# A streaming SiLU-times-multiply kernel: load and store rings exchanged, and the first load issued ahead of the preamble's barrier

## The chip, the cores and the metric

The kernel runs on one core of a Trainium2 chip. The metric is the device time of one execution in microseconds (us).

The engines named are ACT (ScalarE, the SiLU), DVE (VectorE, the multiply) and SP (SyncE, which here only issues DMAs). In the profile, what SP issues is on the ring q1 and what ACT issues on q10: the 134.22 MB of loads are on q1 before, where SP issues them. The profile counts 16 DMA engines. "A DMA engine" below is one of these 16. A transfer has 16 landing records in the trace, which I take as one from each; a packet (one piece of a transfer) has a record of its ring, time and size, but not of the DMA engine that carried it.

## The reference

```python
x: float32 [32, 512, 2048]
x1, x2 = x[..., :1024], x[..., 1024:]
out = x1 * (1 / (1 + np.exp(-x1))) * x2      # float32 [32, 512, 1024]
```

134.2 MB are read and 67.1 MB written.

## The kernel before

The 16,384 rows are cut into 16 tiles of 128 partitions by 8 rows. A tile is loaded by one DMA of 8 MiB, computed in four pieces, and stored by one DMA of 4 MiB. Both pools have two buffers. Loads are issued by SP, stores by ACT. The last tile is stored in four pieces of 1 MiB as its pieces are done. The framework schedules the instructions; it may place those of one engine in another order than the program's.

```python
in_pool  = ctx.enter_context(tc.tile_pool(name="in_pool", bufs=2))
out_pool = ctx.enter_context(tc.tile_pool(name="out_pool", bufs=2))
def load(i):
    xt = in_pool.tile([P, K, in_cols], dt, name="xt")        # K = 8
    nc.sync.dma_start(out=xt, in_=xv[i])                     # L45
    loaded[i] = xt
load(0); load(1)
for i in range(n_tiles):                                     # 16
    ...
    for c in range(0, K, KC):                                # KC = 2
        ce = c + KC
        nc.scalar.activation(out=ot[:, c:ce, :], in_=xt[:, c:ce, :half], func=Silu)    # L56
        nc.vector.tensor_mul(out=ot[:, c:ce, :], in0=ot[:, c:ce, :], in1=xt[:, c:ce, half:])  # L61
        if last:
            nc.scalar.dma_start(out=ov[i][:, c:ce, :], in_=ot[:, c:ce, :])             # L67
    if not last:
        nc.scalar.dma_start(out=ov[i], in_=ot)                                         # L69
    if i + 2 < n_tiles:
        load(i + 2)
```

## Time and profile before

| | before |
|---|---|
| time, median of the first 3 runs | 472.03 us (471.82 to 472.82) |
| span in the profile | 470.1 us |
| bytes moved, mean rate over the span | 201.35 MB, 428 GB/s |
| first load issued / its first packet | 0.73 / 1.73 us |
| load 15 has landed | 451.97 us |
| last store issued / last packet ends / last landing | 465.37 / 468.88 / 469.22 us |

The page of the kernel before: the span, the busy time of the compute engines, the DMA engines' busy tenths in 40 slices, and the rings (packets, MB, share of the 16 engines' span).

```profile
span 470.1 us, 267 instructions
...
DVE 142.4 (30%) x64; ACT 118.3 (25%) x65; POOL 0.2 (0%) x4
...
DMA  8999999999999999999999999999999999999998
...
q1 hardware_dynamic: 2304, 134.22, 66.2%
q10 hardware_dynamic: 2736, 67.11, 33.1%
q14 instruction: 2, 0.02, 0.0%
```

DVE and ACT are busy 30% and 25%; the DMA engines are at nine tenths or more in 38 of 40 slices. Loads are on q1 (SP), stores on q10 (ACT). This kernel is bound by the DMA engines.

The chain of waits that ended last, cut to one period (start, length, what):

```profile
347.05 47.10 DMA xt<-in_x_dram
...
394.23 1.92 ACT ot L56
...
396.18 8.91 DVE ot L61 x4
...
405.10 46.87 DMA xt<-in_x_dram
```

One should not read this as "47 us of load, then 11 us of compute that nobody hides". The next load (405.10) is issued when the compute frees its buffer, but another load is still running then, and so is a store. The chain shows what releases what. That the DMA engines are never empty in the middle is read from the next view: busy shares by stretch (share of the 16 DMA engines and GB/s stand last; a packet is counted whole where it starts, so a share can pass 1).

```profile
core 0: us, DVE busy (x) ACT busy (x) POOL busy (x), PEclk, DMA share, GB/s
60.00:440.00 380.00, 115.67 (x52) 95.02 (x52) 0.00 (x0) 1.00 1.00 434
462.00:464.80 2.80, 1.75 (x1) 1.01 (x1) 0.00 (x0) 1.00 1.01 427
464.80:466.80 2.00, 0.54 (x1) 0.00 (x0) 0.00 (x0) 1.00 0.54 225
466.80:468.90 2.10, 0.00 (x0) 0.00 (x0) 0.00 (x0) 1.00 0.91 375
```

In the 380 us of the middle the share is 1.00 at 434 GB/s. The dip is in the tail: 0.54 in the two microseconds from 464.8.

The timeline of the head (SP issues loads 0 and 1, in one merged line), and of the last tile:

```profile
0.73 0.85 SPq L45 DMA_DIRECT2D xt<-in_x_dram  x2
```

```profile
452.05 5.51 ACT L56 ACTIVATE ot<-xt 128x2048 f32<-128x2048 f32 x3 [21.65 <-DMA xt<-in_x_dram]
453.99 6.70 DVE L61 TENSOR_TENSOR ot<-ot,xt 128x2048 f32<-128x2048 f32 x3 [20.06 <-ACT ot L56]
456.32 4.74 ACTq L67 DMA_DIRECT2D out_dram<-ot  x3
461.11 1.91 ACT L56 ACTIVATE ot<-xt 128x2048 f32<-128x2048 f32 x1 [3.54 <-DVE ot L61]
463.05 2.29 DVE L61 TENSOR_TENSOR ot<-ot,xt 128x2048 f32<-128x2048 f32 x1 [2.36 <-ACT ot L56]
465.37 0.34 ACTq L67 DMA_DIRECT2D out_dram<-ot  x1
```

The framework put three of the last tile's stores between ACT's third and fourth ACTIVATE. Each store waits for a multiply of DVE, so ACT stands still for 3.54 us, DVE then for 2.36 us, and the last store goes out late. ACT's waits say the same:

```profile
ACT ot L56 <- DMA xt<-in_x_dram: 340.4, 16, 21.9
ACT ot L56 <- DVE ot L61: 3.5, 1, 3.5
...
```

### The profile page before, as it was taken

The page shows a single profiled execution, that of the slowest core. Times are in us where ns is not written, and L with a number is a line of the kernel's source. Part 1 is how long each engine was busy: PE and PEld are TensorE (multiplying, and loading weights), DVE is VectorE, ACT ScalarE, POOL GpSimd, SP SyncE. Part 2 cuts the span into 40 slices and gives each one's busy share as a digit, 9 for nine tenths or more (in the row PEclk, how much of TensorE's full clock was granted, in tenths as well). Part 3 has the DMA queues.
Part 4 walks back from the last instruction along what each step waited for, and adds up shares of the span by engine and source line. Part 5 has one row for each costly group of instructions (what it writes and reads, how often), then busy time and mean ns, then how long its engine had stood idle before and what let it go on. Part 6 is the DMA issues. An engine that isn't in the chain of part 4 may idle for free.

```text
span 470.1 us, 267 instructions
## 1 busy us (share of the span) xinstructions
DVE 142.4 (30%) x64; ACT 118.3 (25%) x65; POOL 0.2 (0%) x4
## 2 busy tenths in 40 slices
DVE  0070704207052070511606115070250702407033
ACT  1050506014060240602306032060320604106041
POOL 0000000000000000000000000000000000000000
DMA  8999999999999999999999999999999999999998
GB/s 357 446 446 401 401 485 435 418 401 443 449 446 401 441 457 396 446 474 390 468 404 438 457 441 407 427 420 449 446 410 432 480 401 418 440 474 424 399 424 337
DMA packets 5042, 201.35 MB, mean 428 GB/s; under 512 B 560, under 2 KB 560, under 8 KB 560
## 3 DMA queue, kind: packets, MB, share of 16 engines
q1 hardware_dynamic: 2304, 134.22, 66.2%
q10 hardware_dynamic: 2736, 67.11, 33.1%
q14 instruction: 2, 0.02, 0.0%
HBM read 134.22 MB, written 67.11 MB: 428 GB/s over the span
## 4 chain that ended last, share of the span: by engine, by line
DMA 80%; DVE 15%; ACT 4%; issue 0%; ACTq 0%; SPq 0%
DMA xt<-in_x_dram 80%; DVE ot L61 15%; ACT ot L56 4%; SPq L45 0%; ACTq L67 0%; ACTq L56 0%
## 5 line engine op out<-in xcount | busy, mean ns | idle before, releaser
L61 DVE TENSOR_TENSOR ot<-ot,xt 128x2048 f32<-128x2048 f32 x64 | 142.4, 2286 | 322.9 <-ACT ot L56 322.9
L56 ACT ACTIVATE ot<-xt 128x2048 f32<-128x2048 f32 x64 | 117.1, 1898 | 344.0 <-DMA xt<-in_x_dram 340.4
L56 ACT ACT_TABLE_LOAD x1 | 1.3, 1283 | 0.7 <-PEq L86 0.7
L86 POOL MEMSET const-bfloat16-1.0<- 128x1 bf16 x1 | 0.1, 101 | 0.0
L86 POOL MEMSET const-uint8-127<- 128x1 uint8 x1 | 0.1, 101 | 0.0
L86 POOL MEMSET const-float32-0.0<- 128x1 f32 x1 | 0.1, 98 | 0.2 <-issue 0.2
L86 POOL MEMSET const-float32-1.0<- 128x1 f32 x1 | 0.1, 98 | 0.0
## 6 DMA issues: line engine op xcount, KB each, us to landing
out_dram<-ot ACTq DMA_DIRECT2D x15, 4096.0 KB, 39.7
out_dram<-ot ACTq DMA_DIRECT2D x4, 1024.0 KB, 5.4
xt<-in_x_dram SPq DMA_DIRECT2D x16, 47.1
```

The source lines that it names most:

```text
L56: nc.scalar.activation(out=ot[:, c:ce, :], in_=xt[:, c:ce, :half], func=mybir.ActivationFunctionType.Silu,)
L61: nc.vector.tensor_mul(out=ot[:, c:ce, :], in0=ot[:, c:ce, :], in1=xt[:, c:ce, half:],)
L86: nc = _bacc.Bacc("TRN2", target_bir_lowering=False, num_devices=1)
```

## The change

The program begins with a preamble, which ends in a barrier at which the engines wait for one another (in the trace before, SP and ACT each wait 0.7 us there, for PE last, and go on at 0.65 us); each engine has a drain instruction before it, from 0.00 us (SP) and 0.13 us (ACT) to 0.32 us (PE). The change's intent: (1) start the first transfer before that barrier, (2) take the stores off ACT, so that a store that waits no longer holds up an ACTIVATE. Loads go to ACT, stores to SP, the order is kept as written, and a hook moves the first load ahead of ACT's drain in the preamble. The `PLAN` list only gives every tile the same 8 rows as before.

```diff
+def issue_ahead_of_the_first_barrier(nc):
+    head, body = nc.main_func.blocks[:2]
+    load = next(ins for ins in body.instructions if type(ins).__name__ == "InstDMACopy")
+    at = next(
+        j for j, ins in enumerate(head.instructions)
+        if ins.engine == load.engine and type(ins).__name__ == "InstDrain"
+    )
+    body.instructions = [ins for ins in body.instructions if ins.name != load.name]
+    head.instructions = head.instructions[:at] + [load] + head.instructions[at:]
...
+    nc.at_finalize(issue_ahead_of_the_first_barrier)
+    ctx.enter_context(tc.manual_schedule())
...
-        nc.sync.dma_start(out=xt, in_=xv[i])
+        nc.scalar.dma_start(out=xt[:, :plan[i][1], :], in_=view(x_flat, i))
...
-                nc.scalar.dma_start(out=ov[i][:, c:ce, :], in_=ot[:, c:ce, :])
+                nc.sync.dma_start(out=ov[:, c:ce, :], in_=ot[:, c:ce, :])
...
-            nc.scalar.dma_start(out=ov[i], in_=ot)
+            nc.sync.dma_start(out=ov, in_=ot[:, :k, :])
```

More of the change, by code (lines that the diff above doesn't have):

```diff
@@ L31, with view @@
     KC = 2
-    n_tiles = num_rows // (P * K)
-    assert n_tiles * P * K == num_rows
+    PLAN = [K] * (num_rows // (P * K))
     in_pool = ctx.enter_context(tc.tile_pool(name="in_pool", bufs=2))
     out_pool = ctx.enter_context(tc.tile_pool(name="out_pool", bufs=2))
-    xv = x_flat.rearrange("(n p k) d -> n p k d", p=P, k=K)
-    ov = out_flat.rearrange("(n p k) d -> n p k d", p=P, k=K)
+    plan = []
+    row = 0
+    for k in PLAN:
+        plan.append((row, k))
+        row += P * k
+    assert row == num_rows
+    n_tiles = len(plan)
+    def view(flat, i):
+        row0, k = plan[i]
+        return flat[row0:row0 + P * k].rearrange("(p k) d -> p k d", k=k)
+    nc.at_finalize(issue_ahead_of_the_first_barrier)
+    ctx.enter_context(tc.manual_schedule())
     loaded = {}
@@ L50 @@
     for i in range(n_tiles):
+        k = plan[i][1]
         xt = loaded.pop(i)
         last = i == n_tiles - 1
+        ov = view(out_flat, i)
         ot = out_pool.tile([P, K, half], dt, name="ot")
-        for c in range(0, K, KC):
-            ce = c + KC
+        for c in range(0, k, KC):
+            ce = min(c + KC, k)
             nc.scalar.activation(
```

## The prediction

0.6 us (head) and 1.1 us (tail) make 1.7 us, and 472.03 − 1.7 gives 470.3 us.

> **What bounds the kernel now.** The DMA engines. The page shows 201.35 MB at a mean of 428 GB/s, DMA share 9 in 38 of 40 slices, DVE busy 30%, ACT 25%. The chain of waits alternates: a load of 46.9 to 47.2 us, 10.9 us of compute (one ACTIVATE of 1.92, four multiplies, 8.91), the next load: 58.05 us for two tiles, or 25.17 MB: 433.5 GB/s. [...] A new load always queues behind one still running (issued at 405.10 us, the previous lands at 423.0), and a store is always queued too (39.7 us to landing, one every 29 us). So neither ring runs dry between head and tail.
>
> Only the two ends are not full (timeline and DMA packet records):
> - Head: barrier released at 0.65 us; first load issued by SP at 0.73; first packet at 1.73.
> - Tail: load 15 lands at 451.97. ACT runs three ACTIVATEs, then stands behind three stores that it issues itself and that wait for DVE (456.32 to 461.06), and starts the fourth only at 461.11. DVE idles 2.36 us; the last store is issued at 465.37. The DMA engines finish their backlog at about 465.3 and run half empty for 2 us (7.4 and 10.1 of 16 active), 0.9 us lost. The last packet ends at 468.88, lands at 469.22; 0.9 us of epilogue follows.
>
> **What the change does.**
> 1. First load ahead of the barrier: ACT's preamble drain stands at 0.13 us, so the load is issued there instead of at 0.73: 0.6 us earlier. The barrier may come up to 0.4 us later and the table load (1.28 us) may stand before load 1; both hide under the 20 us of load 0. As the middle is DMA-bound, the 0.6 us go through to the end.
> 2. Stores on SP: in the tail ACT no longer stands behind stores. Four ACTIVATEs back to back, DVE without its gap: last store 2.4 us earlier after the last landing. Only the DMA gap is won: the last 1 MiB follows the backlog directly. Estimate from the packets: 0.9 to 1.2 us.
> 3. Loads on ACT: load i+2 waits for the last multiply of tile i, 2.4 us after ACT's last ACTIVATE, then 0.33 us of issue; ACT idles 20 us there anyway. Nothing.
> 4. Exchange of rings: [...] no change of rate expected.
>
> Sum: 0.6 + 1.1 = 1.7 us of 472.03, so **470.3 us, range 469.0 to 472.0**. Faster by over 2%: 0.01, within 2%: 0.97, slower by over 2%: 0.02. Over 2% faster would need under 462.6 us, and 201.3 MB at 433.5 GB/s alone take 464.4.
>
> **What would show it.** Step 1: first load issued at 0.1 to 0.2 us, packets from about 1.1, landing near 22.1 instead of 22.73. Step 2: in the last 20 us four ACTIVATEs in 7.3 us, no idle of DVE among the four multiplies, last store about 11 us after load 15 lands, no dip of the DMA share before the last packets. Steps 3 and 4: load 15 lands at about 451.4, two tiles still per 58.05 us, ACT still waiting for loads.
>
> **What would make it wrong.** [...] loads could get another share beside stores, so that load 15 lands earlier or later, or the rate drifts (1% would be 4.7 us). An early issue that starts no packet sooner. Automatic and hand order differing in waits.

## The result and the profile after

The changed kernel takes 470.78 us in the median (470.65 to 470.98, 4 runs) against 472.16 (471.82 to 472.82, 4 runs) beside it: ratio 0.997, 95% interval 0.9952 to 0.9987. A ratio here is the mean time of one kernel's fast runs over that of the other's of the same rounds, so not quite the ratio of the medians. A ratio of 0.001 is 0.47 us. Within 2% it is "same", but the interval lies below 1: a small, real gain. Two later measurements of the same kernel gave 0.9976 and 0.9982. So the change is worth 0.85 to 1.4 us.

The page after:

```profile
span 468.9 us, 269 instructions
...
DVE 142.3 (30%) x64; ACT 118.2 (25%) x65; POOL 0.2 (0%) x4
...
DMA  9899999999999998999999999999999989999998
...
q10 hardware_dynamic: 2304, 134.22, 66.4%
q1 hardware_dynamic: 2736, 67.11, 33.2%
q14 instruction: 2, 0.02, 0.0%
```

The rings have changed places (loads now on q10, stores on q1). The busy times are as they were; the DMA engines are at nine tenths or more in 36 of the 40 slices (38 before).

The chain, one period:

```profile
346.08 47.15 DMA xt<-in_x_dram
...
393.26 1.92 ACT ot L87
...
395.20 8.91 DVE ot L92 x4
...
404.13 46.88 DMA xt<-in_x_dram
```

A period of two tiles is 404.13 − 346.08 = 58.05 us, exactly as before (405.10 − 347.05). The middle is untouched.

Head, tail, the tail's stretches and ACT's waits after:

```profile
0.13 1.13 ACTq L74 DMA_DIRECT2D xt<-in_x_dram  x2
```

```profile
451.03 7.31 ACT L87 ACTIVATE ot<-xt 128x2048 f32<-128x2048 f32 x4 [21.57 <-DMA xt<-in_x_dram]
452.97 8.90 DVE L92 TENSOR_TENSOR ot<-ot,xt 128x2048 f32<-128x2048 f32 x4 [19.98 <-ACT ot L87]
455.29 6.94 SPq L98 DMA_DIRECT2D out_dram<-ot  x4
```

```profile
60.00:440.00 380.00, 115.65 (x52) 95.01 (x52) 0.00 (x0) 1.00 1.00 432
460.80:463.60 2.80, 1.06 (x1) 0.00 (x0) 0.00 (x0) 1.00 1.01 427
463.60:465.60 2.00, 0.00 (x0) 0.00 (x0) 0.00 (x0) 1.00 1.02 430
465.60:467.70 2.10, 0.00 (x0) 0.00 (x0) 0.00 (x0) 1.00 0.64 269
```

```profile
ACT ot L87 <- DMA xt<-in_x_dram: 338.8, 16, 22.1
...
```

The first load is issued at 0.13 us and its first packet starts at 1.14 us, 1.0 us after the issue, as before (0.73 to 1.73). Four ACTIVATEs follow each other in 7.31 us, the multiplies have no gap, ACT never waits for DVE, and the stretch from 463.6 us has a share of 1.02 where before had 0.54. But the last stretch is now poorer than before (0.64 against 0.91). Part of the hole has moved to the end, and this is where the forecast saving of the tail went.

Landing and packet records show what happened. The 16 landings of a transfer do not come together: those of load 15 came between 450.72 (first engine) and 451.97 us (last engine) before. I call this difference, 1.25 us, the lag, and read it as DMA engines that are not abreast. What waits for a transfer waits for the last of them: ACT's first ACTIVATE on load 15 starts at 452.05 us.

- Before, the last store but one landed between 465.33 and 466.50 us. A landing follows its packets' end by 0.34 us (469.22 − 468.88 at the very end), so the fastest engine was free at about 464.99 and the slowest at about 466.16. The last store's packets started at 466.21 to 466.36. So the slowest engine had almost no gap, 0.05 to 0.2 us (the packet records themselves: the last packet of the backlog ends at 466.14); the hole was on the fast ones. Its 16 landings then lie within 0.15 us: the late issue had given all engines a common start.
- After, no engine waits, the lag stays, and the last store's landings spread over 0.79 us (467.17 to 467.96).

Idle of the DMA engines from 450 us to the last packet, averaged over the 16 (from the packet records): 1.00 us before, 0.57 after. The end moved by less than that, since the slowest engine sets it.

The end of the last packet moved by 468.88 − 467.62 = 1.25 us in the two profiled runs. It splits into 0.59 (first packet: 1.727 to 1.138), 0.38 (load 15's last landing came 0.97 earlier, of which 0.59 is the head; the rest is a smaller lag, 0.89 instead of 1.25 us) and 0.29 (from load 15's last landing to the last packet's end: 16.91 to 16.62).

### The profile page after: what moved, and what is told of

Its sections match the earlier page's. It is cut to its first block, busy times and chain, and to the rows that moved or that the text cites. A ratio compares the mean times of both kernels' runs of the same rounds, so it can differ in the third digit from the quotient of the medians.

```text
span 468.9 us, 269 instructions
## 1 busy us (share of the span) xinstructions
DVE 142.3 (30%) x64; ACT 118.2 (25%) x65; POOL 0.2 (0%) x4
## 4 chain that ended last, share of the span: by engine, by line
DMA 80%; DVE 15%; ACT 3%; DVEq 0%; issue 0%
DMA xt<-in_x_dram 80%; DVE ot L92 15%; ACT ot L87 3%; DVEq L128 0%
```

## The experiments

My theory (A, the prediction): the head's 0.6 us go through, and the mean idle of the tail's gap, 0.9 to 1.2 us, is won. Rivals: (B) the slowest DMA engine sets the end, so the tail gives only a few tenths, and the rest of the first measurement's 1.4 us is lag that differs from run to run; (C) the exchange of rings itself shrinks the lag. Two more (D, E) came up on the way. Each call ran on one chip beside its own runs of the kernel before (median 472.08, 471.89 and 472.33 us). All results were correct.

All runs in one table, read from instruction, landing and packet records of one trace each. "Tail" is from load 15's last landing to the end of the last packet. "8 KB" is the total time of the last tile's 512 packets of 8 KB, divided by 16 engines. Times in us.

| run | first issue | first packet | load 15: first engine | last engine | lag | tail | 8 KB | ratio to before |
|---|---|---|---|---|---|---|---|---|
| before | 0.73 | 1.73 | 450.72 | 451.97 | 1.25 | 16.91 | 9.95 | |
| changed | 0.13 | 1.14 | 450.12 | 451.00 | 0.89 | 16.62 | 9.89 | 0.9970 |
| e1 early only | 0.00 | 1.00 | 450.10 | 451.73 | 1.63 | 16.90 | 9.99 | 0.9987 |
| e2 tail only | 0.73 | 1.75 | 450.71 | 452.44 | 1.73 | 16.70 | 10.16 | 0.9999 |
| e3 early and tail | 0.00 | 1.00 | 450.13 | 451.15 | 1.02 | 16.79 | 10.37 | 0.9983 |
| e4 changed, not early | 0.73 | 1.75 | 450.99 | 451.98 | 0.99 | 16.73 | 9.89 | 0.9993 |
| e5 changed again | 0.13 | 1.15 | 450.14 | 451.13 | 0.99 | 16.61 | 9.89 | 0.9976 |
| e6 changed, old tail | 0.13 | 1.13 | 450.12 | 451.15 | 1.03 | 16.84 | 10.41 | 0.9984 |
| e7 before, by hand | 0.73 | 1.72 | 450.93 | 452.02 | 1.09 | 21.81 | 10.08 | 1.0103 |
| e8 fewer instructions | 0.00 | 1.00 | 448.93 | 451.72 | 2.79 | 17.49 | 10.57 | 0.9989 |
| e9 changed, third | 0.12 | 1.15 | 450.29 | 451.42 | 1.12 | 16.71 | 9.89 | 0.9982 |
| e10 store amid loads | 0.00 | 1.00 | 450.38 | 453.87 | 3.49 | 16.23 | 10.11 | 1.0014 |
| e11 small early store | 0.12 | 1.15 | 450.42 | 451.44 | 1.03 | 16.70 | 9.91 | 0.9976 |
| e12 tiles in one piece | 0.12 | 1.14 | 447.76 | 448.88 | 1.12 | 19.14 | 9.89 | 0.9984 |

The 95% interval of each ratio is about ±0.0013, or 0.6 us, so single times can hardly rank these kernels; the trace columns do the work. Landing and tail of e8, e10 and e12 are not to be set beside the others: in these three the middle was altered, and the loads end earlier or with a much larger lag.

### e1: the early issue alone

The kernel before, with the same hook; its first load is on SP, whose drain stands at 0.00 us.

```diff
+    nc.at_finalize(issue_ahead_of_the_first_barrier)
```

> The kernel before with only its first load (on SP, as before) issued ahead of the barrier. SP's drain stands at 0.00 us, so the issue should start there instead of at 0.73: 0.7 us earlier, first packet at about 1.0 instead of 1.73. Theory A (my prediction: the head's saving goes through a DMA-bound middle undiminished): load 15 lands, on the first of its 16 DMA engines, 0.7 us earlier, and the time falls by 0.7 us. Theory B (the 16 engines drift apart; what ends a load is the slowest engine, and most of the change's 0.97 us at load 15 is a drift that differs from run to run): first engine's landing 0.7 us earlier as well, the last engine's anywhere from 0.3 to 1.1 us earlier. Theory C (the exchange of rings is what shrinks the spread between engines, 1.25 us to 0.89 at load 15): here, with rings as before, the spread stays at 1.2 us or more.

Measured: 471.53 us (470.99 to 471.69), ratio 0.9987 (0.9974 to 1.0000), about 0.6 us faster, at the edge of the noise. The first packet came 0.73 us earlier, the first engine's landing of load 15 0.62 us earlier, the last engine's only 0.24 earlier, since this trace has a lag of 1.63. The head's saving arrives nearly whole at the fastest engine's landing of load 15, as A and B both say; the last engine's figure is what B says. It is also what C says of the spread here, which e3 answers.

### e2: the tail alone

```diff
             if last:
-                nc.scalar.dma_start(out=ov[i][:, c:ce, :], in_=ot[:, c:ce, :])
+                nc.sync.dma_start(out=ov[i][:, c:ce, :], in_=ot[:, c:ce, :])
```

> The kernel before with only the four stores of the last tile moved from ACT to SP; rings otherwise as before, no early issue. The fourth ACTIVATE should follow the third, DVE should lose its 2.36 us gap, and the last store should be issued about 11.0 us after load 15 lands instead of 13.4. Theory A (my prediction: the DMA engines' mean idle of 0.9 us in the gap is what is won): last packet's end 0.9 to 1.2 us sooner after load 15's last landing than before (16.9 us). Theory B (the gap lies on the fast engines only; the slowest engine, 1.2 us behind, went through it almost without a stop, and it sets the end): only 0.2 to 0.4 us sooner, that is 16.5 to 16.7 us, the last store's 16 landings spread over 0.8 us or more instead of 0.15, and a time 0.2 to 0.5 us below before.

Measured: 472.00 us (471.74 to 472.22), ratio 0.9999 (0.9985 to 1.0012): nothing that can be seen. The instructions did what was wanted (four ACTIVATEs in 7.31 us, last store 10.95 us after load 15 instead of 13.40), the tail is 16.70 instead of 16.91 us, and the last store's landings spread over 1.50 us instead of 0.15. Theory A falls: it asked for 0.9 to 1.2 us. B's 0.2 to 0.4 us in the trace is met; its time, 0.2 to 0.5 us below, is not confirmed.

### e3: both, with the rings not exchanged

```diff
 (the edits of e1 and e2 together)
```

> Both of the above, rings not exchanged otherwise: loads stay on SP, stores of tiles 0 to 14 on ACT. If the exchange itself does nothing, this should equal the change or beat it by about 0.13 us (SP reaches its drain 0.13 us before ACT): 1.0 to 1.6 us below before. If the exchange matters (theory C), the spread of load 15's landings is 1.2 us or more here, and the saving is 0.3 to 0.4 us less than the change's 1.4.

Measured: 471.20 us (470.90 to 471.65), ratio 0.9983 (0.9971 to 0.9996), 0.8 us faster. The lag at load 15 is 1.02 us with the rings as before, and it was 0.29 to 0.50 us up to load 10. So a small lag does not need the exchange; C in its strong form falls. Yet the median gain stays short of the 1.0 to 1.6 us expected (the interval, 0.2 to 1.4 us, does not exclude them).

A possible reason is in the tail. The stretch from 457.0 to 458.5 us, in which the first pieces of the last tile go out, first in e3, then in e5 (the changed kernel again, below), where the stores have a ring of their own and load 15 lands at the same time (451.15 and 451.13 us); columns as above, share and GB/s last:

```profile
457.00:458.50 1.50, 1.50 (x2) 1.50 (x1) 0.00 (x0) 1.00 0.90 240
```

```profile
457.00:458.50 1.50, 1.50 (x2) 1.47 (x1) 0.00 (x0) 1.00 0.88 371
```

In e3 the engines are busy 0.90 of the time for 240 GB/s, 267 per full share; in e5 0.88 for 371, or 422. With each packet's bytes spread over its own time, the rate in the three half microseconds from 457.0 us is 302, 249 and 319 GB/s in e3, and 428, 427 and 428 in e5. In e3 ten 8 KB packets took 0.57 to 1.38 us there instead of 0.31. The time of the 8 KB packets sorts the runs: 10.16 to 10.57 us in the four (e2, e3, e6, e8) that put the last tile's stores on a ring that had carried only loads until then, and 9.89 to 10.08 in the nine traces in which they go on the ring of all other stores (e10, between the two, is taken up below). So the DMA engines spend 0.3 to 0.7 us more on these packets than in the changed kernel, in the mean of the 16, where the last tile's stores go on the ring of the loads. Exchanging the rings for all tiles avoids that. I had not thought of this merit of the exchange.

In the time of the kernel it is not shown. All of e3's slow packets start between 457.02 and 457.36 us, on engines that came free early, and by theory B such engines have time to spare: the tails of e2, e3 and e6 (16.70 to 16.84 us) are 0.0 to 0.2 us longer than those with the stores on one ring throughout (16.61 to 16.73), and the times do not tell them apart. Nor is the cause shown. A turn from loads to stores is not enough: in e10, below, SP's ring makes one in the middle of the run without a slow packet. What the four runs also have in common is that the store before the last tile's is still running, on the other ring, when the slow packets start; whether that matters, no run here tests.

### e4: the change without the early issue

```diff
-    nc.at_finalize(issue_ahead_of_the_first_barrier)
```

> The change without its early issue: rings exchanged, order by hand. First load issued by ACT just after the barrier at about 0.7 us, first packet at about 1.7. Theory A: 1.1 us below before, since the tail is worth that. Theory B: 0.3 us below before, give or take 0.4 for drift. Theory C: spread at load 15 about 0.9 us rather than 1.25, and 0.6 to 0.7 us below before.

Measured: 471.50 us (471.47 to 472.23), ratio 0.9993 (0.9980 to 1.0005), 0.3 us faster, which is within the noise; tail 16.73 us. This is B's figure; A's 1.1 us lies just outside the interval. Together with e1 (0.6 us) it makes 0.9, which agrees with what the change measured on the same chip later (e9: 0.85 us), though each of the three figures is known only to 0.6 us.

### e5: the changed kernel once more

> The changed kernel once more, unaltered, for a second trace and times beside the others of this call. Theory B (the slowest of the 16 DMA engines sets the end, and how far it lags varies from run to run): the first engine's landing of load 15 again at 450.1 us (within 0.1), but the lag of the last one differs from 0.89 us by some tenths. Theory C (lag belongs to the kernel): 0.89 again, within 0.1. Time 0.9 to 1.4 us below before.

Measured: 470.79 us (470.61 to 470.85), ratio 0.9976 (0.9963 to 0.9988). The first engine's landing repeats to 0.03 us (450.14), the lag differs by 0.10 us (0.99); a third trace (e9) had 1.12. So the lag of one kernel does vary, though in this pair it varied little; earlier in the run it varied more (load 9: 0.53, 0.48 and 1.55 us in the three traces).

### e6: the change with the tail's old order

The last tile's stores are put back on ACT, in the order that the framework had chosen before. The edit, shortened:

```diff
+        for j in cs[:3]: chunk(*j)            # ACTIVATE and multiply
+        if last:
+            for j in cs[:3]: store(*j)        # nc.scalar.dma_start
+        chunk(*cs[3])
+        if last: store(*cs[3])
```

> The change with its loads on ACT, its early issue and its stores of tiles 0 to 14 on SP, but the last tile's four stores on ACT in the order of the kernel before: three ACTIVATEs, three stores, the fourth ACTIVATE, the fourth store. The last store should be issued 13.4 us after load 15 lands instead of 10.9. Theory A (tail worth 0.9 to 1.2 us): 1.0 us slower than the changed kernel of this call. Theory B (the late issue only reaches the point at which the slowest engine is free, so it costs 0.1 to 0.3 us): 0.1 to 0.3 us slower, last packets ending 16.9 us after load 15's last landing, its 16 landings within 0.2 us of one another.

Measured: 471.04 us (470.98 to 471.47), ratio 0.9984 against 0.9976 for e5 on the same chip: 0.4 us slower than the changed kernel (all five runs lie above e5's five, which end at 470.85). The last store was issued 13.35 us after load 15, the tail is 16.84 us, the landings lie within 0.15 us. This is B, with A's 1.0 us excluded by the trace (0.23 us). The slow packets are here too, now on ACT's ring (8 KB packets 10.41 us), so not all of the 0.23 us need come from the late issue:

```profile
457.00:458.50 1.50, 1.50 (x2) 0.00 (x0) 0.00 (x0) 1.00 0.91 251
```

### e7: the kernel before in the order as written

```diff
+    ctx.enter_context(tc.manual_schedule())
```

> The kernel before with its instruction order kept as written and nothing else changed: ACT then stands behind each of the last tile's stores, so the last store is issued about 18.2 us after load 15 lands (four times 1.92 + 2.29 + 0.34 with the short waits, less the last issue). Theory B with the threshold that I read from the trace: end of packets = issue + 0.85 + 2.66 us wherever the issue comes later than the slowest engine's backlog, that is 21.7 us after load 15's last landing instead of 16.9: 4.8 us slower than before. A rival in which the DMA backlog still hides most of it expects under 2.5 us. This places the knee: the tail of the kernel before sits just at it, so that advancing its last store gains little and delaying it costs in full.

Measured: 476.82 us (476.64 to 476.87, 4 runs), ratio 1.0103 (1.0090 to 1.0117), 4.9 us slower; the tail is 21.81 us where 21.7 was expected. Its last tile:

```profile
452.10 1.91 ACT L58 ACTIVATE ot<-xt 128x2048 f32<-128x2048 f32 x1 [21.57 <-DMA xt<-in_x_dram]
454.04 2.29 DVE L63 TENSOR_TENSOR ot<-ot,xt 128x2048 f32<-128x2048 f32 x1 [19.98 <-ACT ot L58]
456.37 0.34 ACTq L69 DMA_DIRECT2D out_dram<-ot  x1
456.75 1.91 ACT L58 ACTIVATE ot<-xt 128x2048 f32<-128x2048 f32 x1 [2.74 <-DVE ot L63]
...
470.32 0.34 ACTq L69 DMA_DIRECT2D out_dram<-ot  x1
```

Each ACTIVATE now stands behind the store of the piece before. The last store is issued at 470.32 us, 18.30 after load 15. This places the kernel before: advancing its last store by 2.4 us (13.40 to 10.95 or 10.89) gains 0.2 to 0.3 us in the trace, delaying it by 4.9 us costs 4.9. It stood at the knee, where the issue meets the slowest engine just coming free.

It also says that "stores on ACT" and "order by hand" do not go together here. The change could take the order as written only because no store is left on ACT. The exchange of rings in the framework's own order was not run.

### e8: fewer instructions

Theory D, a guess: two 8 KB packets of the queue that the profile calls "instruction" (q14), of 0.31 us each, at 290 to 314 us, each hold up one DMA engine. Packet records do not name the engine, and what these packets are for is not shown. The lag of the changed kernel went from 0.53 us (load 9) to 1.06 (load 11) there. The data packet right after each (in these two traces it starts 3 ns before the q14 packet ends) was slow in every trace so far: 1.33 and 1.57 us instead of 1.21 for a 32 KB store in the changed kernel, 2.74 and 2.98 instead of 2.42 for a 64 KB load in the one before.

```diff
-        for c in range(0, K, KC):
-            ce = c + KC
+        step = KC if last else 4
+        for c in range(0, K, step):
+            ce = c + step
```
(on top of e3)

> Early issue and tail stores on SP (rings not exchanged), with tiles 0 to 14 computed in two pieces instead of four: 60 fewer instructions in the middle. In the traces so far two 8 KB packets of the queue for instructions run at 290 to 314 us, and in three of six traces the lag of the slowest DMA engine jumps there by 0.5 to 0.9 us. Theory D [...]: with about half the instructions none of them falls in the span, there is no jump, the lag at load 15 is 0.6 us or less, and the time is 0.3 to 0.8 us below the run of early issue and tail alone (so 1.2 to 1.7 us below before). Rival: the lag comes from elsewhere; then it is 0.9 to 1.7 us again, and the time about 0.8 us below before.

Measured: 471.18 us (470.79 to 472.27), ratio 0.9989 (0.9976 to 1.0001). The packets moved to 456.0 us and the lag had no jump in the middle, but one engine fell 2.79 us behind at load 1 and stayed there, and the profile fell on the slowest of the five runs. No gain; D's time is not confirmed.

### e9: the changed kernel a third time

> The changed kernel a third time, as the yardstick on this chip: 0.9 to 1.4 us below before, time of the last tile's 512 packets of 8 KB 9.9 us per engine as in both earlier traces (9.89).

Measured: 471.18 us (471.10 to 472.15), ratio 0.9982 (0.9969 to 0.9994), 8 KB packets 9.89 us. It is the yardstick of e10 to e12.

### e10: one store in the middle of the loads' ring

On top of e3, tile 5 is stored by SP, to see whether it is a ring's first store (E1) or each turn from loads to stores (E2) that costs.

```diff
-            nc.scalar.dma_start(out=ov[i], in_=ot)
+            q = nc.sync if i == 5 else nc.scalar
+            q.dma_start(out=ov[i], in_=ot)
```

> Early issue and last tile's stores on SP, rings not exchanged, and the store of tile 5 on SP too, so that SP's ring has carried a store before the tail. In the traces so far the DMA rate drops for 1.5 to 3 us wherever a ring carries its first store (to about 315 GB/s for 3 us at store 0 in every trace; to 250 to 320 GB/s for 1.5 us at 457 us where the tail's ring had carried only loads), and the 8 KB packets then took 10.2 to 10.6 us per engine instead of 9.9. Theory E1 (the cost is that of a ring's first store of all): a dip after tile 5's store at about 180 us, none at 457 us, 8 KB packets 9.9 to 10.0. Theory E2 (each turn of a ring from loads to stores costs it): dips at both places, 8 KB packets 10.2 to 10.6. Time 0.4 to 1.0 us below before in either.

Measured: 473.02 us (472.44 to 473.50), ratio 1.0014 (1.0002 to 1.0027), a miss for both theories. The store stands in line between loads 6 and 7; the lag of the loads' landings went from 0.48 us (load 6) to 3.53 (load 8) and stayed, to 3.49 at load 15, and at 458 us the DMA engines ran nearly empty (1 to 4 of 16 active for 1.4 us) because load 15 was complete so late. The 8 KB packets took 10.11 us, but on engines that had run dry, so this does not decide between E1 and E2. Tile 5's store does, and against both: its packets run from 186.2 to 195.1 us, on SP's ring, which carried no store before and turns from a load to it; each takes its usual 1.21 to 1.23 us, and with each packet's bytes spread over its own time the rate stays at 432 to 435 GB/s from 180 to 195 us. So neither a ring's first store nor its turn from loads to stores is by itself the cause. (No store ran on ACT's ring meanwhile, so the case named at the end of e3 is not tested.) What the cause is stays open. What the run also shows: one store in the loads' line costs 1.5 us more than e3's arrangement (1.0014 against 0.9983 on the same chip, in different calls).

### e11: a small store early

In every trace the rate falls to about 300 to 330 GB/s for 3 us just before the first store's packets start, from 36 us in most (0.9 us lost), and never at a later store on the same ring. The slow packets are the loads': in the changed kernel 16 of them, of 64 KB, take 3.2 to 3.4 us instead of 2.42, while the store's own take their usual 1.21. In e12, below, whose first store comes later, the dip comes later too, at 40.5 us. Can a small store take this dip in advance?

```diff
+    small = small_pool.tile([P, 128], dt, name="small")
+    nc.vector.memset(small, 0.0)
     load(0)
     load(1)
+    nc.sync.dma_start(out=view(out_flat, 0)[:, 0, :128], in_=small)
```

> The changed kernel with one extra store of 64 KB of zeros, issued on SP's ring at about 1 us into rows of tile 0 that tile 0's own store overwrites later. Theory E1: the dip to 315 GB/s for 3 us at 36 us (about 0.9 us lost) is gone there; the small store takes its dip during the first packets of load 0, which run slow anyway (3.05 us instead of 2.42). If the two slow spells overlap, the time falls by 0.5 to 0.9 us against the changed kernel; if they add up, it is the same within 0.3 us. Theory E2 or a cost of large stores: the dip stays at 36 us and the time is 0.2 us above the changed kernel for the added bytes.

Measured: 471.21 us (471.09 to 471.29), ratio 0.9976 (0.9964 to 0.9989), beside e9's 471.18. The dip at 36 us is still there (314 GB/s from 37 to 39 us). A small first store does not take it, so E1 falls here too. The cause of this dip is open.

### e12: tiles in one piece

The changed kernel with tiles 0 to 14 computed in one piece.

```diff
-        for c in range(0, k, KC):
-            ce = min(c + KC, k)
+        step = KC if last else k
+        for c in range(0, k, step):
+            ce = min(c + step, k)
```

> The changed kernel with tiles 0 to 14 computed in one piece instead of four, 90 fewer instructions. Theory D (the two 8 KB instruction packets at 294 and 312 us each hold up one DMA engine, by 0.31 us of their own and 0.12 to 0.54 us on the packet after them): none of them in the span, no jump of the lag of the slowest engine after 290 us (it went from 0.5 to 1.06 and 1.11 us there), lag of the last store but one under 0.6 us instead of 0.8 to 0.9, time 0.3 to 0.6 us below the changed kernel. Rival (the lag has other causes): lag 0.8 us or more and no gain; and if the longer compute per tile (16.3 us instead of 10.9) makes a ring run dry, several us slower.

Measured: 471.60 us (471.09 to 471.87), ratio 0.9984 (0.9970 to 0.9997); no gain on e9. No instruction packet falls in the span, and the lag has no jump at 290 to 315 us. But it grew in small steps from 0.57 us (load 2) to 1.12 (load 15), and the last store but one had a lag of 1.14. So without the instruction packets there is no jump, in this as in e8; with them there is one of about 0.4 to 0.9 us in six of the twelve other traces (changed, e3 to e7), and of 0.2 us or less in the rest. Doing without them won no time. D as a way to save time falls. No version that I ran beats the changed kernel clearly.

## Why the prediction was right or wrong, point by point

- **Bound by DMA, "same" within 2%, time within 469.0 to 472.0: right.** 470.78 us against 470.3 forecast; the middle kept its 58.05 us per two tiles.
- **Step 1, the early issue, 0.6 us: right in mechanism and size.** Issue at 0.13, packets from 1.14 us, 0.59 earlier; the first engine's landing of load 15 came 0.61 us earlier. Alone it was worth about 0.6 us (e1). Over the traces with an unaltered middle, the first engine's landing of load 15 is at 450.19 us in the mean of seven with the early issue and at 450.84 in the mean of four without, 0.65 us apart. The landing of load 0 came 0.87 earlier and not 0.6, since it is the slowest engine's, whose lag differed.
- **Step 2, the tail, "0.9 to 1.2 us": right in mechanism, three to six times too large.** ACTIVATEs, multiplies and issue came as said, and the dip before the last packets went. But I took the mean idle of 16 engines for the saving. The slowest engine had 0.05 to 0.2 us of idle before the last store, and it sets the end. The tail became 0.29 us shorter in the first pair of traces, and 0.2 to 0.3 over all traces of the changed kernel (16.61 to 16.71 against 16.91, and 16.90 in e1, which has the same tail).
- **Steps 3 and 4, loads on ACT and the exchange: right for the middle, incomplete for the tail.** I expected that the exchange does nothing, which no trace had then shown. The rate in the middle agrees (434 and 432 GB/s). But where a ring took its first stores in the tail, its packets took 0.3 to 0.7 us more per DMA engine than in the changed kernel, and the exchange spares the tail this; that it shortens the kernel is not shown.
- **The sum, 1.7 us.** Measured 1.4, 1.1 and 0.85 us in three measurements. In the first pair of traces, 0.38 us of the 1.25 are a smaller lag. That was no step of mine, and it is why load 15 landed at 451.00 and not at the 451.4 that I forecast; it made the prediction look better than its second term was, which was luck. Whether the exchange makes the lag smaller on average is open: 1.02 to 1.73 us at load 15 in the five traces before, e1, e2, e3, e7 with loads on SP (2.79 in e8), and 0.89 to 1.12 in the seven traces with loads on ACT. The ranges overlap, but four of these six lie above all seven, so theory C in a weak form stands as a rival for these tenths.

## What to carry to other kernels

In this kernel, whose DMA engines were full from 60 to 440 us (share 1.00, 434 GB/s), only the two ends were left to win. Cost a gap in the tail on the slowest DMA engine, not on their mean: here the mean idle of 0.9 to 1.2 us was forecast as the saving, the slowest engine had 0.05 to 0.2 us of it, and the tail gained 0.2 to 0.3. What an earlier or later store was worth here depended on the moment at which that engine was free: 2.4 us earlier gained 0.2 to 0.3 us, 4.9 us later cost 4.9 (e7). The spread of a transfer's 16 landings (1.25 us at load 15 before) warned that the mean would mislead. Take waiting stores off an engine that still has to compute (ACT stood still for 3.54 us), and if you do so, do it for the whole kernel: putting only the last tile's stores on the loads' ring made their packets slower here (10.16 to 10.57 us per DMA engine against 9.89 to 10.08), though a cost in time was not shown; and when measuring a change of one microsecond, take several traces, since a lag that differs by some tenths (0.89 to 1.12 us at load 15 in three traces of the changed kernel) looks just like a gain.
